# The shift and scale columns of the first norm, summed on TensorE in four column groups of the array

## The chip, the core and the metric

The kernel runs on one of the eight cores of a Trainium2 chip. A core has TensorE (matrix products, PE in the profile; its weight loads are PEld), VectorE (DVE), ScalarE (ACT), GpSimd (POOL) and SyncE (SP, which here only issues transfers), on-chip memory of 128 partitions (SBUF), a memory of eight banks per partition into which TensorE writes its products (PSUM), and 16 DMA engines that bring data from the chip's main memory. The metric is the device time of one execution in microseconds (us); less is better.

## The reference

A trunk of two residual layers over 256 tokens of 2048 features, in float32. The first layer mixes with a gated MLP over chunks of tokens beside a convolution, the second with attention; each then has an MLP of 8192 hidden channels. Every norm is modulated by a conditioning vector c:

```python
c_act = jax.nn.silu(c)
for l in range(DEPTH):
    mod = c_act @ ada_w[l] + ada_b[l]          # [2048] @ [2048, 12288]
    shift1, scale1, gate1, shift2, scale2, gate2 = jnp.split(mod, 6, axis=-1)
    h = _modulate(_rms(x, norm1_g[l]), shift1, scale1)   # rms * (1 + scale) + shift
    mix = _even_mixer(h, ...) if l % 2 == 0 else _mla_mixer(h, ...)
    x = x + gate1 * mix
    h = _modulate(_rms(x, norm2_g[l]), shift2, scale2)
    x = x + gate2 * (square(relu(h @ mlp_w1[l])) @ mlp_w2[l])
```

Each of the six vectors of a layer is a product of one row with 2048 x 2048 of ada_w, 16 MiB of weights that are used once. This document is about shift1 and scale1 of the first layer: nothing of the first mixer's projection can start without them.

## The kernel before

**Weights.** `wraw` (lines 111 to 122) loads a tile of 512 rows by 512 columns, 1 MiB, as four blocks of 128 rows on the 128 partitions, on SyncE's queue. Tiles for conditioning lie in the pool `raw` (four buffers), tiles that are multiplied as whole float32 (`gemm32`, lines 147 to 156) in `wh` (three buffers).

**Conditioning.** `ada_quarters` (lines 246 to 276) makes two columns side by side, shift (j0) and scale (j0 + 1), 512 features at a time: a quarter is eight steps, each with one tile. A step has four product-sums on VectorE, one for each block of 128 rows (lines 267 and 269): the accumulator `accq` [128, 512] gets the block times the 128 values of c that belong to it, one to a partition. After four tiles of a column `ada_finish_col` (lines 216 to 223) has to sum `accq` over the partitions: TensorE transposes its four blocks of 128 columns into PSUM (`transpose4`, lines 102 to 108), VectorE reduces them along the free axis (line 221) and adds the bias (line 223). The result is feature-major: 128 features on the partitions, four columns for a quarter.

**The first stage** (`even`, lines 474 to 505). Four steps are issued, then x is loaded and its squares summed by ScalarE (`setup_x`, lines 897 to 905), two more steps, then `setup_vectors` (lines 907 to 918), which transposes small vectors (biases, norm gains) that ScalarE's queue has loaded as rows (`vr`, lines 877 to 893). `tc.issue_after(self.last)` queues instructions of the block behind the named one where they run on its engine. When a quarter of the columns is there, `norm_start`'s generator gives, for both halves of the tokens, the normed x transposed (line 355) with the shift and gain columns, and ScalarE writes the modulated, transposed features (line 500). Then three tiles of the projection are multiplied (lines 503 to 505): 24 float32 products a quarter, 128 x 128 by 128 x 512. In the profile their outputs are called mm and pa.

**Order.** A framework orders the instructions of each engine by the program and by its own estimate of readiness, and sets all waits. While `gemm32` asks for a weight tile, `side_work` (lines 135 to 145) takes steps off the conditioning queue, here 8/3 to a tile; so a quarter's three weight tiles are followed by two, three and three steps for the next quarter, ahead of the tile's products in the program. `ada_until` takes as many as are still wanting.

PSUM has four buffers for products (`mm`), two for transposes and small things (`tr`) and two more (`ms`).

After this stage come the rest of the projection (`gemm32` too), with the gate of the first mixer and the next shift and scale computed beside it, and then the rest of the trunk.

Of the kernel before, what the change touches and what calls it, by code (L numbers as in the profile page):

```python
# [9 lines left out]
F32 = mybir.dt.float32  # L10
# [3 lines left out]
ALU = mybir.AluOpType  # L14
AX = mybir.AxisListType

P = 128
D = 2048
T = 256
NH = T // P  # L20
KB = D // P
# [21 lines left out]
class Trunk:  # L43
    def __init__(self, ctx, tc, t):
# [17 lines left out]
        self.first = 0  # tiles still to be split by GpSimd  # L62
# [5 lines left out]
    def rsqrt(self, out, v):  # L68
        """out = v ** -0.5 for v > 0: a first guess from the bits, a third-order step, a Newton step."""
# [14 lines left out]
        # out <- 8/3 of its third-order step, then Newton with the 8/3 taken out again  # L84
# [7 lines left out]
    def split(self, src, hi, lo, engine=None):  # L92
        """src = hi + lo, both with the 12 significant bits that one pass of the array takes."""
        self.nc.scalar.copy(hi, src)  # L94
        (engine or self.nc.vector).tensor_tensor(lo, src, hi.bitcast(F32), op=ALU.subtract)  # L95
# [6 lines left out]
    def transpose4(self, srcs):  # L102
        """Up to four [128, n] blocks -> one PSUM bank, transposed side by side."""
        ps = self.tr.tile([P, 512], F32, tag="tr", name="trp")
        for i, s in enumerate(srcs):
            w = s.shape[-1]
            self.nc.tensor.transpose(ps[:w, i * P : i * P + s.shape[0]], s, self.ident[: s.shape[0], : s.shape[0]])  # L107
        return ps

# [14 lines left out]
    def wtile(self, w, k0, nk, n0, nw):  # L124
# [3 lines left out]
        # VectorE is busy with the norm when a phase's first tiles come: GpSimd splits those  # L128
# [6 lines left out]
    def side_work(self, size=1.0):  # L135
        """Work that is spread beside the weight tiles: conditioning and the convolution."""
# [10 lines left out]
    def gemm32(self, ps, x, w, g, n0):  # L147
        """ps += x[:, 512 features of group g] @ w[those, n0:n0+512], whole float32 passes."""
# [12 lines left out]
    def gemm(self, x, xk0, w, k0, nkb, n0, nw, skew=False):  # L161
        """[256, nw] = x[:, K] @ w[K, n0:n0+nw], as two PSUM tiles of 128 tokens; with skew the
        first half of the tokens is complete well before the second."""
# [25 lines left out]
    def gemm_quarter(self, units, x, q, paired):  # L189
        """512 features of x into each of units = (psum, w, n0, nw); with paired, the first half of  # L190
        the tokens of two units goes before their second half."""
# [23 lines left out]
    # mod = silu(c) @ ada_w + ada_b, one 1 MiB piece of ada_w to a step  # L215
    def ada_finish_col(self, out, layer, j, q, acc):
        """Feature-major column sums of acc [128, 512], plus the bias."""
# [7 lines left out]
    def ada_col(self, layer, j):  # L225
        """self.mod[layer, j] = [128, 16], feature-major."""
# [19 lines left out]
    def ada_quarters(self, layer, j0, side=None, aided=0):  # L246
        """Columns j0 and j0 + 1 side by side, complete for 512 features after every eight steps.
        The first aided quarters go by ScalarE and GpSimd, with room for products in side."""
# [28 lines left out]

    def ada_row(self, layer, j, side=None):
        """self.mod[layer, j] = [128, 2048], the same in every partition. With side = [128, 4096],
        the products go to ScalarE and the sums to GpSimd."""  # L280
# [37 lines left out]
    def at_end(self, last):  # L318
        """Before the last product of a stage: no more work beside it."""
        self.hold = last  # L320
        return last

    def ada_more(self, rate, *lists):
        """Steps to be worked off beside the coming weight tiles, rate steps to a tile."""
        for l in lists:
            self.ada_queue.extend((rate, step) for step in l)
# [24 lines left out]
    def norm_t(self, h, q, r):  # L351
        """Four blocks of (x * r).T in PSUM."""
# [4 lines left out]
    def norm_start(self, layer, which):  # L357
        """A function that gives 512 features' (shift, gain) columns: modulate(rms(x) * g) = x * rstd * gain + shift."""
# [14 lines left out]
    def norm_quarter(self, quarter, q, pair):  # L373
        """512 features of h.T, as (hi, lo)."""
# [10 lines left out]
    def norm_mod(self, layer, which):  # L385
        """h.T (hi, lo) of modulate(rms(x) * g, shift, scale)."""
# [6 lines left out]
    def gated(self, src, gate, h, c):  # L393
        """x[:, chunk] += gate * src, for one half"""
# [6 lines left out]
    def residual(self, ps, gate, c, last, part=None):  # L401
        """x[:, chunk] += gate * (ps + part)"""
# [16 lines left out]
    def mlp(self, layer, last):  # L419
# [8 lines left out]
        # the first three chunks take the features as the modulation completes them  # L428
# [9 lines left out]
        # sums over the blocks of hidden channels  # L438
# [35 lines left out]
    def even(self, layer):  # L474
# [5 lines left out]
        self.ada_more(8 / 3, self.ada_quarters(layer, 0))  # L480
        self.ada_steps(X_AT)
        self.setup_x()
        self.ada_steps(V_AT - X_AT)
        with self.tc.issue_after(self.last):
            self.setup_vectors()
# [3 lines left out]
        # mixer B  # L489
# [34 lines left out]
        def glu(j, pa, pg):  # L524
# [8 lines left out]
            def tap(b, k):  # L533
                # read from PSUM, which leaves GpSimd its port to SBUF
# [9 lines left out]
            # two sums side by side, so that no tap waits on the one before  # L544
# [11 lines left out]
        # mixer A  # L556
# [46 lines left out]
        def layer_norm():  # L603
            """LayerNorm over channels (the partition axis), swish."""
# [24 lines left out]
        # mixer A's rows of the first three chunks, then mixer B's  # L629
# [18 lines left out]
    def rms_columns(self, srcs):  # L648
        """1 / rms along the free axis of each of some [128, n], as the columns of one tile."""
# [18 lines left out]
    def low_rank(self, src, r, gcol, pair, k0, h):  # L668
        """One half's [128, 512], scaled by its rms r and by g, transposed and split."""
# [11 lines left out]
    def rope(self, out, src, tab, n):  # L681
        """Rotary pairs of [128, n, 64]; tab = [128, 128]: (C1 | C2), (-S2 | S1)."""
# [8 lines left out]
    def odd(self, layer):  # L691
# [12 lines left out]
        # columns 512:1088 = c_kv and the rotary key, as pieces of 320 and 256 columns  # L704
# [21 lines left out]
        # two heads at a time: keys, values and queries, then scores, then the output, a step apart  # L726
# [10 lines left out]
        def squares(c, s, src):  # L737
            """Sums of squares of [P, half, head, n], as row s of three."""
# [20 lines left out]
        def normalized(c):  # L759
# [8 lines left out]
            # rotary pairs of both halves  # L768
# [16 lines left out]
        def scores(c):  # L785
# [3 lines left out]
            for i in range(2):  # L789
                rows = slice(i * ROPE, (i + 1) * ROPE)  # L790
                sc = self.ms.tile([P, 512], F32, tag="ms", name="sc")
                # query block 1 sees 256 keys, query block 0 the first 128
# [18 lines left out]
        def weights_t(ss):  # L811
            out = []
            for s in ss:
                # transposed: keys 0..127 for query blocks 0 and 1, keys 128..255 for block 1
# [45 lines left out]
    def setup(self):  # L860
# [9 lines left out]
        nc.vector.tensor_copy(self.cT, ps[:, :KB])  # L870
        one = self.tmp.tile([P, P], F32, tag="t512", name="one")
# [4 lines left out]
        # 128-long rows that become per-partition columns  # L876
# [43 lines left out]
    def setup_even(self):  # L920
        nc, t, c = self.nc, self.t, self.const
        # conv taps: rows (tap, block) -> columns
# [12 lines left out]
        # spatial weights, lower triangle, transposed  # L935
# [10 lines left out]
    def setup_odd(self, room):  # L946
        """Mask and rotary tables, with room [128, 768] for the raw ones."""
        nc, t = self.nc, self.t
        # causal mask: query block 1 on 256 keys, then query block 0 on 128
# [9 lines left out]
        # rotary tables of both halves with the head gains  # L959
# [39 lines left out]
def rope_table():  # L999
    """cos | sin of the rotary angles, [256, 64]: by shape alone."""  # L1000
# [23 lines left out]
```

## Time and profile before

| what | value |
|---|---|
| device time, median of three runs | 2189.13 us |
| lowest and highest | 2187.72, 2189.61 us |
| span of the profiled execution | 2185.9 us |
| TensorE busy (products), share | 2090.9 us, 96% |
| VectorE busy, share | 1564.9 us, 72% |
| ScalarE busy, share | 932.3 us, 43% |
| GpSimd busy, share | 146.7 us, 7% |
| data moved | 567.70 MB, mean 260 GB/s |

The profiled execution's own device time is not listed apart from its span. The span runs from the first instruction to the last; the median of the runs is 3.2 us above it, launch and end included.

How to read the rows. A row of the timeline gives start, length in us, engine, line, operation, output<-inputs, how many instructions are merged in it, and in brackets the idle time before it and what ended that. SPq and ACTq are the queues that issue transfers. A row of the groups gives line, engine, operation, names, shapes and count, then busy time, the mean of one in ns, and the idle time just before with what ended it. `PE` records of products overlap: a record ends later than the next one starts, so a rate is read from starts. Some of the first page's rows, in 40 equal slices of 54.6 us, show the first stage in the first two or three digits:

```profile
PE   2889999899999999999998999989999999999999
DVE  6849999888777878787767878766656545554555
DMA  9999968899898899989755646647778556556653
GB/s 350 384 346 330 332 242 295 275 317 339 315 337 315 329 326 319 339 304 334 270 174 174 211 158 214 229 154 250 256 271 264 178 192 189 189 192 192 189 191 122
```

### The profile page before, as it was taken

How to read it: one execution, taken by the hardware profiler on the slowest of the kernel's cores; microseconds unless marked ns; L12 is line 12 of the kernel's file. 1: busy time of each engine (PE TensorE's matmuls, PEld its weight loads, DVE VectorE, ACT ScalarE, POOL GpSimd, SP SyncE). 2: the span in 40 equal slices, each digit the busy share in tenths (PEclk: the TensorE clock that was granted, in tenths of full speed). 3: DMA queues.
4: the chain of work that ended last, by engine and by line, in shares of the span. 5: the costliest groups of instructions: out<-in, count | busy, mean ns of one | idle time of the engine just before them, and what ended most of it. 6: DMA issues, size and time to landing. Idle time of an engine off the chain costs nothing.

```text
span 2185.9 us, 23655 instructions
## 1 busy us (share of the span) xinstructions
PE 2090.9 (96%) x9138; PEld 1635.7 (75%) x9138; DVE 1564.9 (72%) x1763; ACT 932.3 (43%) x1184; POOL 146.7 (7%) x95
## 2 busy tenths in 40 slices
PE   2889999899999999999998999989999999999999
PEld 1444458678888888888888787868888888888887
DVE  6849999888777878787767878766656545554555
ACT  2135435444444334333436776444434433433432
POOL 0038710000000000000001000010000000000000
PEclk9999999899999999999999999989999999999999
DMA  9999968899898899989755646647778556556653
GB/s 350 384 346 330 332 242 295 275 317 339 315 337 315 329 326 319 339 304 334 270 174 174 211 158 214 229 154 250 256 271 264 178 192 189 189 192 192 189 191 122
DMA packets 238620, 567.70 MB, mean 260 GB/s; under 512 B 9150, under 2 KB 17784, under 8 KB 221864
## 3 DMA queue, kind: packets, MB, share of 16 engines
q1 hardware_dynamic: 236288, 562.60, 74.3%
q10 hardware_dynamic: 1564, 2.28, 0.3%
q8 instruction: 72, 1.18, 0.2%
q0 software_dynamic: 656, 1.31, 0.2%
q14 instruction: 40, 0.33, 0.0%
HBM read 564.06 MB, written 2.10 MB: 259 GB/s over the span
## 4 chain that ended last, share of the span: by engine, by line
PE 85%; DVE 9%; DMA 5%; ACT 1%; issue 1%; SPq 0%; ACTq 0%; DVEq 0%
PE mm L183 23%; PE mm L184 23%; PE mm L185 23%; PE mm L153 4%; DMA raw<-in_ada_w 4%; PE trp L107 3%; DVE accq L269 2%; DVE cvsq L542 1%; DVE wl L95 1%; PE mm L210 1%; PE mm L211 1%; PE mm L212 1%; PE sc L797 1%; PE sc L796 1%; DMA raw<-in_mlp_w 1%
## 5 line engine op out<-in xcount | busy, mean ns | idle before, releaser
L95 DVE TENSOR_TENSOR wl<-raw,wh 128x2048 fp32r<-128x2048 f32 (+2 forms) x312 | 704.7, 2259 | 424.0 <-PE mm L184 317.9
L94 ACT CAST wh<-raw 128x2048 fp32r<-128x2048 f32 (+3 forms) x316 | 596.6, 1888 | 774.1 <-PE mm L185 515.2
L183 PE MATMUL mm<-wh,f_h 128*128 128x512 f32 x1024 | 399.6, 390 | 0.0
L185 PE MATMUL mm<-wh,f_l 128*128 128x512 f32 x1024 | 399.3, 390 | 0.0
L184 PE MATMUL mm<-wl,f_h 128*128 128x512 f32 x1024 | 398.7, 389 | 0.0
L185 PE MATMUL mm<-wh,h_l 128*128 128x512 f32 (+2 forms) x928 | 358.2, 386 | 0.0
L183 PE MATMUL mm<-wh,h_h 128*128 128x512 f32 (+2 forms) x928 | 358.2, 386 | 0.0
L184 PE MATMUL mm<-wl,h_h 128*128 128x512 f32 (+2 forms) x928 | 357.0, 385 | 0.6 <-DVE wl L95 0.6
L185 PEld LDWEIGHTS mm<-wh,f_l 128*128 128x128 f32 x1024 | 192.2, 188 | 39.8
L184 PEld LDWEIGHTS mm<-wl,f_h 128*128 128x128 f32 x1024 | 192.3, 188 | 39.6
L183 PEld LDWEIGHTS mm<-wh,f_h 128*128 128x128 f32 x1024 | 192.3, 188 | 39.2
L184 PEld LDWEIGHTS mm<-wl,h_h 128*128 128x128 f32 x928 | 175.0, 189 | 34.0 <-DVE wl L95 1.1
L185 PEld LDWEIGHTS mm<-wh,h_l 128*128 128x128 f32 x928 | 174.9, 188 | 33.4
L183 PEld LDWEIGHTS mm<-wh,h_h 128*128 128x128 f32 x928 | 175.0, 189 | 32.7
L153 PE MATMUL mm<-raw,x 128*128 128x512 f32 x448 | 195.7, 596 | 1.0 <-ACT x L500 0.6
L269 DVE SCALAR_TENSOR_TENSOR accq<-raw,cT,accq 128x512 f32<-128x512 f32 x210 | 153.7, 749 | 16.6 <-DMA raw<-in_ada_w 13.3
L153 PEld LDWEIGHTS mm<-raw,x 128*128 128x128 f32 x448 | 84.6, 191 | 104.6 <-issue 98.5
L237 DVE SCALAR_TENSOR_TENSOR acc<-raw,cT,acc 128x2048 f32<-128x2048 f32 x60 | 140.8, 2346 | 9.7 <-DMA raw<-in_ada_w 9.7
L297 DVE SCALAR_TENSOR_TENSOR acc<-raw,cT,acc 128x2048 f32<-128x2048 f32 x48 | 112.7, 2347 | 4.4 <-DMA raw<-in_ada_w 4.4
L542 DVE SCALAR_TENSOR_TENSOR cvsq<-yp,convw,cvsq 128x256 f32<-128x256 f32 x240 | 96.0, 476 | 0.0
L303 POOL TENSOR_TENSOR side<-side 128x1024 f32<-128x1024 f32 x32 | 74.8, 2361 | 19.3 <-ACT side L302 19.3
L452 ACT ACTIVATE relu<-mm 128x512 f32<-128x512 f32 x60 | 35.8, 599 | 87.7 <-PE mm L185 81.5
(270 smaller groups left out, 2246.9 us busy)
## 6 DMA issues: line engine op xcount, KB each, us to landing
raw<-in_mlp_w SPq DMA_DIRECT2D x256, 1024.0 KB, 5.6
raw<-in_ada_w SPq DMA_DIRECT2D x192, 1024.0 KB, 5.4
raw<-in_ab_w_in SPq DMA_DIRECT2D x32, 1024.0 KB, 9.7
raw<-in_ab_w_out SPq DMA_DIRECT2D x16, 1024.0 KB, 8.3
raw<-in_mla_w_out SPq DMA_DIRECT2D x16, 1024.0 KB, 4.9
raw<-in_mla_w_ukv SPq DMA_DIRECT2D x8, 1024.0 KB
raw<-in_mla_w_uq SPq DMA_DIRECT2D x8, 768.0 KB, 4.8
raw<-in_mla_w_in SPq DMA_DIRECT2D x4, 1024.0 KB, 7.2
```

The source lines that it names most:

```text
L94: self.nc.scalar.copy(hi, src)
L95: (engine or self.nc.vector).tensor_tensor(lo, src, hi.bitcast(F32), op=ALU.subtract)
L107: self.nc.tensor.transpose(ps[:w, i * P : i * P + s.shape[0]], s, self.ident[: s.shape[0], : s.shape[0]])
L153: self.nc.tensor.matmul(ps[h], x[:, 4 * g + k, h * P : (h + 1) * P], raw[:, k, :], start=g + k == 0, stop=4 * g + k == KB - 1,)
L183: nc.tensor.matmul(o, a, hi[:, i, :nw], start=first, stop=False)
L184: nc.tensor.matmul(o, a, lo[:, i, :nw], start=False, stop=False)
L185: nc.tensor.matmul(o, b, hi[:, i, :nw], start=False, stop=last)
L237: nc.vector.scalar_tensor_tensor(acc, raw, self.cT[:, kb : kb + 1], acc, op0=ALU.mult, op1=ALU.add)
L269: self.last = nc.vector.scalar_tensor_tensor(acc, raw[:, k, :], c, acc, op0=ALU.mult, op1=ALU.add).ins
L297: nc.vector.scalar_tensor_tensor(acc, raw, c, acc, op0=ALU.mult, op1=ALU.add)
L303: nc.gpsimd.tensor_tensor(acc[:, sl], acc[:, sl], prod, op=ALU.add)
L542: nc.vector.scalar_tensor_tensor(o, y, wk, o, op0=ALU.mult, op1=ALU.add)
```

## The change

The new `ada_quarters_pe` takes the place of `ada_quarters` for the first layer's first two columns; other uses of `ada_quarters` stay. In a step TensorE multiplies each of the four blocks of 128 rows with its 128 values of c, repeated into 32 columns, and writes to 32 partitions of one PSUM bank: block k of every tile goes to partitions 32k to 32k + 31. The four tiles of a column accumulate there. Then ScalarE copies the bank to SBUF, TensorE multiplies each block of 128 columns with a vector `sel` that is one on partitions 0, 32, 64 and 96 (this adds the four groups and turns the features onto the partitions), and VectorE adds the bias. The steps of a column now follow each other (`q, i, g` in place of `q, g, i`). `setup_vectors` is called first, since the bias add needs it, and `issue_after` names ScalarE's copy. `sel` is a sum over the identity's columns 0, 32, 64 and 96.

```diff
+    def ada_quarters_pe(self, layer, j0):
+        nc = self.nc
+        box = {}
+
+        def step(q, i, g):
+            if (q, i, g) == (0, 0, 0):
+                for j in (j0, j0 + 1):
+                    self.mod[layer, j] = self.const.tile([P, KB], F32, tag=f"mod{layer}{j}", name=f"mod{layer}{j}")
+            if g == 0:
+                box["acc"] = self.tr.tile([P, 512], F32, tag="tr", name="adap")
+            acc = box["acc"]
+            raw = self.wraw(self.t["ada_w"][layer], 4 * g, 4, (j0 + i) * D + q * 512, 512)
+            for k in range(4):
+                rows = slice(32 * k, 32 * k + 32)
+                nc.tensor.matmul(acc[rows], self.cT[:, 4 * g + k : 4 * g + k + 1].broadcast_to([P, 32]), raw[:, k, :], start=g == 0, stop=g == 3)
+            if g == 3:
+                rows = self.tmp.tile([P, 512], F32, tag="t512", name="adar")
+                self.last = nc.scalar.copy(rows, acc).ins
+                ps = self.tr.tile([P, 512], F32, tag="tr", name="adac")
+                for k in range(4):
+                    nc.tensor.matmul(ps[:, k : k + 1], rows[:, k * P : (k + 1) * P], self.sel, start=True, stop=True)
+                b0 = layer * 96 + (j0 + i) * KB + 4 * q
+                nc.vector.tensor_tensor(
+                    self.mod[layer, j0 + i][:, 4 * q : 4 * q + 4], ps[:, :4], self.ada_b[:, b0 : b0 + 4], op=ALU.add
+                )
+                if i == 1:
+                    self.quarters[layer, j0] = q + 1
+
+        self.quarters[layer, j0] = 0
+        return [lambda q=q, g=g, i=i: step(q, i, g) for q in range(4) for i in range(2) for g in range(4)]
...
     def even(self, layer):
...
-        self.ada_more(8 / 3, self.ada_quarters(layer, 0))
+        self.setup_vectors()
+        self.ada_more(8 / 3, self.ada_quarters_pe(layer, 0))
         self.ada_steps(X_AT)
         self.setup_x()
-        self.ada_steps(V_AT - X_AT)
-        with self.tc.issue_after(self.last):
-            self.setup_vectors()
         self.ada_until(lambda: self.quarters[layer, 0] > 0)
...
     def setup(self):
...
         nc.vector.tensor_copy(self.cT, ps[:, :KB])
+        self.sel = c.tile([P, 1], F32, name="sel")
+        nc.vector.tensor_reduce(self.sel, self.ident.rearrange("p (a b) -> p a b", b=32)[:, :, 0], axis=AX.X, op=ALU.add)
```

## The prediction

> **What bounds the kernel now.** I read the page first, then the busy windows of its first 170 us, then TensorE's timeline there, because the change touches nothing later.
>
> ```profile
> span 2185.9 us, 23655 instructions
> PE 85%; DVE 9%; DMA 5%; ACT 1%; issue 1%; SPq 0%; ACTq 0%; DVEq 0%
> raw<-in_ada_w SPq DMA_DIRECT2D x192, 1024.0 KB, 5.4
> ...
> 50.00:60.00 10.00, 10.00 (x25) 4.40 (x24) 9.68 (x15) 0.00 (x0) 0.00 (x0) 1.00 1.05 387
> 60.00:70.00 10.00, 7.01 (x20) 3.13 (x18) 9.43 (x15) 0.00 (x0) 0.00 (x0) 1.00 1.05 387
> 80.00:90.00 10.00, 7.16 (x17) 2.85 (x15) 8.01 (x11) 0.00 (x0) 0.00 (x0) 1.00 1.05 387
> 110.00:120.00 10.00, 7.02 (x16) 2.84 (x16) 7.50 (x11) 0.00 (x0) 0.00 (x0) 1.00 1.05 387
> 130.00:140.00 10.00, 9.29 (x30) 4.76 (x31) 1.03 (x4) 3.11 (x9) 1.55 (x2) 1.00 0.93 330
> ```
>
> The chain that ended last is 85% TensorE; over the whole span this is a TensorE kernel. In a window row stand the stretch and its length, then the busy time of PE, PEld, DVE, ACT and POOL, PE's granted clock, the DMA share and GB/s. In the four rows up to 120 us the DMA engines are full at 387 GB/s, VectorE is busy for 75 to 97% and TensorE has idle time. One tile of 1024 KB takes 1.049 MB / 387 GB/s = 2.71 us. A quarter of the features needs eight tiles of ada_w and three of ab_w_in: 11 x 2.71 = 29.8 us.
>
> ```profile
> 45.24 14.46 PE L153 MATMUL mm<-raw,x 128*128 128x512 f32 x32
> ...
> 72.75 14.41 PE L153 MATMUL mm<-raw,x 128*128 128x512 f32 x32
> 90.57 6.25 PE L153 MATMUL pa<-raw,x 128*128 128x512 f32 x10 [3.41 <-DMA raw<-in_ab_w_in]
> ...
> 102.32 7.13 PE L153 MATMUL mm<-raw,x 128*128 128x512 f32 x16 [0.29 <-ACT x L500]
> ...
> 120.72 6.26 PE L153 MATMUL pa<-raw,x 128*128 128x512 f32 x10 [3.71 <-DMA raw<-in_ab_w_in]
> 126.82 0.60 PE L107 MATMUL trp<-ident,accq 128*128 128x128 f32 x4
> 127.25 2.74 PE L153 MATMUL pa<-raw,x 128*128 128x512 f32 x6
> ...
> 132.45 14.00 PE L153 MATMUL mm<-raw,x 128*128 128x512 f32 x32 [0.29 <-ACT x L500]
> 146.29 7.03 PE L153 MATMUL pa<-raw,x 128*128 128x512 f32 x16
> 153.25 0.33 PE L107 MATMUL trp<-ident,cwr 62*128 62x62 f32 x2
> ```
>
> The four quarters start their products at 45.24, 72.75, 102.32 and 132.45: the last two periods are 29.6 and 30.1 us, the DMA's 29.8. TensorE waits 3.4 and 3.7 us for weights in the two middle ones. So in this stage the transfers set the pace, VectorE comes next, and TensorE has slack. From 132.45 on it has none:
>
> ```profile
> 190.00:210.00 20.00, 20.00 (x48) 8.85 (x47) 19.92 (x52) 10.96 (x13) 18.49 (x10) 1.00 0.90 328
> ```
>
> Whatever moves the end of the fourth quarter's products (now 153.25) moves the rest of the kernel with it, since TensorE is then full, and VectorE's convolution starts from these products too.
>
> **The change part by part.** *Removed from VectorE:* 128 product-sums, and eight reductions of transposed sums.
>
> ```profile
> L269 DVE SCALAR_TENSOR_TENSOR accq<-raw,cT,accq 128x512 f32<-128x512 f32 x120 | 88.2, 750 | 16.0 <-DMA raw<-in_ada_w 13.3
> L153 PE MATMUL mm<-raw,x 128*128 128x512 f32 x448 | 195.7, 596 | 1.0 <-ACT x L500 0.6 <-DMA raw<-in_ab_w_in 0.4
> L153 PE MATMUL pa<-raw,x 128*128 128x512 f32 x64 | 32.0, 654 | 7.1 <-DMA raw<-in_ab_w_in 7.1
> 51.39 0.19 PEld L153 LDWEIGHTS mm<-raw,x 128*128 128x128 f32 x1 [0.24 <-issue]
> 51.82 0.19 PEld L153 LDWEIGHTS mm<-raw,x 128*128 128x128 f32 x1 [0.24 <-issue]
> ```
>
> That is 88 us of VectorE for 120 of them, all beside transfers. Its worth is the delay between the last tile's landing and the first product, counted below; the 30 us period itself does not shrink.
>
> *Added to TensorE.* Line 153 calls 32 tiles x 8 = 256 float32 products, and has 448 + 64 = 512 records: a product is two passes, each with its own weight load, started 0.43 us apart (51.39, 51.82). A quarter's 24 products are 48 passes and take 153.25 - 132.45 = 20.8 us. The new sum has 4 products of the same 512 columns in a step, 32 a quarter: 64 passes. Only 32 columns of the array are used by each, but a pass streams the same 512 columns of data. No row of before has two passes side by side, so the price has two ends:
> - all one after another, as the passes of line 153: 64 x 0.43 = 27.5 us a quarter;
> - all four column groups at once: 16 x 0.43 = 6.9 us.
>
> I take a value between. The two passes of one product fall on the same columns and must follow each other; the queue holds both passes of the first group, then both of the second. If a pass cannot start before the one ahead of it in the queue (no row here shows one overtaking), the second group's first pass runs beside the first group's second, and so on: two passes at a time, 32 x 0.43 = 13.8 us. A run of steps also has an unpaired pass at its end; at 8/3 steps to a weight tile there are three runs a quarter: 1.3 us.
>
> The Trainium skill, "TensorE: Matmul & The Clock Gate", Part 3, says that matmuls in different column groups overlap, with starts about 4 ns apart, that three groups gave 2.38 times, and that matmuls start and end strictly in program order. By its span formula alone a step would cost little more than its two passes, the first rival below with its 2187 to 2191 us; by its order rule, with the two passes that line 153 shows, it is the pairing and 2216 us. No row of before shows either. "TensorEngine Tiling (Array Packing)", Tiling Modes, speaks against the change: a change of the tiling mode drains TensorE, and here there would be six changes a quarter. The trace of before has no such change to time; if each cost the 0.16 us by which a record of line 153 (596 ns) outlasts its 0.43, three quarters would be 2.9 us longer, 2219 us.
>
> *The new finish* of a column: ScalarE's copy out of PSUM, four products with one column, a bias add.
>
> ```profile
> L520 ACT COPY a<-mm 128x512 f32<-128x512 f32 x2 | 1.1, 588 | 0.1
> 39.19 0.16 DVE L223 TENSOR_TENSOR mod<-mod,ada_b 128x4 f32<-128x4 f32 x1
> 42.34 0.16 DVE L367 SCALAR_TENSOR_TENSOR A<-mod,vecs 128x4 f32<-128x4 f32 x1
> 44.63 0.81 ACT L500 ACTIVATE x<-trp,mod,A 128x128 f32<-128x128 f32 x2 [17.83 <-PE trp L107]
> ```
>
> The four products are eight passes, each with a full 128-column weight load as a transpose has it; four transposes pass in 127.25 - 126.82 = 0.43 us, so 0.107 us a pass, 0.86 us a column, 1.7 us a quarter. They replace eight transposes (0.86 us). The eight transposes of x stay: 0.86 us. The added wait is TensorE's for the copy: 0.59 us and two handovers, twice a quarter. Behind it in TensorE's queue stand the next steps and products of weight tiles, which VectorE and ScalarE wait for. Nothing prices it exactly: between nothing, where products of a weight tile are placed in it, and 2 us a quarter. I take 1.2 us, for this and for idle time where the array's shape changes. The two PSUM buffers that sums, finish and transposes now share lie in the same 0 to 2 us.
>
> *The start.* What decides it is when the eighth tile lands.
>
> ```profile
> 6.73 0.48 DVE L267 TENSOR_SCALAR accq<-raw,cT 128x512 f32<-128x512 f32 x1 [1.63 <-DMA raw<-in_ada_w]
> 11.33 0.49 DVE L267 TENSOR_SCALAR accq<-raw,cT 128x512 f32<-128x512 f32 x1 [3.32 <-DMA raw<-in_ada_w]
> 13.83 9.56 SPq L118 DMA_DIRECT2D raw<-in_ada_w  x4
> 39.31 0.75 DVE L269 SCALAR_TENSOR_TENSOR accq<-raw,cT,accq 128x512 f32<-128x512 f32 x1
> ...
> 10.00:12.00 2.00, 0.00 (x0) 0.01 (x1) 0.67 (x2) 0.30 (x1) 0.00 (x0) 1.00 0.19 69
> 12.00:14.00 2.00, 0.73 (x3) 0.45 (x3) 2.00 (x4) 0.00 (x0) 0.00 (x0) 1.00 0.73 201
> 14.00:16.00 2.00, 0.00 (x0) 0.00 (x0) 0.46 (x1) 0.00 (x0) 0.00 (x0) 1.00 1.05 400
> 12.02 0.73 PE L107 MATMUL trp<-ident,vr 106*128 106x106 f32 x3 [7.13 <-DMA vr<-in_mla_kv_norm_g]
> SPq L118 <- DMA raw<-in_ada_w: 9.1, 1, 9.1
> ```
>
> SyncE waits 9.1 us for a landing, and there is a hole in the transfers up to about 13.8 us. Two tiles of ada_w have landed by then (VectorE opens their sums at 6.73 and 11.33). I see nothing that would fill the hole, so six tiles and the two of x follow: 13.8 + 8 x 2.71 = 35.5 us. Before, VectorE was still summing at 39.3 and the first product started at 45.24. After: 35.5 + the last step's rest 0.9 + copy 0.6 + finish 1.1 + bias add and gain 0.3 + activation 0.5 + about 1.4 of handovers = 40.3 us. The row statistics are ready by then, since VectorE is idle. So 4.9 us are won here.
>
> *Moved:* setup_vectors goes ahead of the sums: three transposes, two copies, one small product, no DMA. On TensorE's queue the sums now stand behind the transposes, which wait for vr until 12.02; the first tile lands near 6.7, so the first step starts near 12.8. Its buffer comes free at 13.7 to 16.2, against SyncE's 13.83 for the fifth tile's issue; the tiles of x, which need no such buffer, lie between and keep the queue filled. I cost it at nothing; without that cover it would be up to 2.4 us. The column selector's reduction is some 0.2 us on an idle VectorE: nothing.
>
> *Sum.* A quarter on TensorE: 20.8 + 13.8 + 1.3 + 1.7 + 0.9 + 1.2 = 39.7 us, more than the DMA's 29.8: TensorE becomes the bound of the stage. End of the fourth quarter: 40.3 + 3 x 39.7 + 20.8 = 180.2, against 153.25: 26.9 us later. The span becomes 2212.8; the median of 2189.13 is 3.2 above the span, and I keep that: **2216 us**. With 0 to 2 us for waits and 0 to 0.1 us of extra per pair, this case is 2209 to 2229.
>
> **The rivals.**
> *All four groups at once (it does not get slower).* For it: the four groups share neither columns nor output partitions. Against it: each has two passes, and the second group's come behind both of the first's. The quarter is 20.8 + 6.9 + 1.7 + 0.9 + 1.2 = 31.5, or 30.3 without waits; with the first product at 39.5 the end is 151.2 to 154.8, 2187 to 2191 us: the start's gain is paid back, nothing is left. It decides from a step of about 0.9 us. It cannot do much better, since 29.8 is the DMA's floor: 39.5 + 89.4 + 20.8 = 149.7, 2185.6.
> *The groups don't run at once (the change doesn't do what it says).* For it: every row of before has one pass after another. Then a step is 3.43 us, more than the DMA's 2.71; the eighth tile's step ends at 40.9, the first product starts at 45.5, a quarter is 20.8 + 27.5 + 1.7 + 0.9 + 1.2 = 52.1, the end 45.5 + 156.3 + 20.8 = 222.6: 2258 us, up to 2266 with waits.
>
> **How the numbers follow.** Two at a time 0.55, one at a time 0.26, all at once 0.13, 0.06 for other orders of work that I have not seen (halved between the signs). The range 2197 to 2266 leaves out four at once and little else. Two executions differ by up to 2 us and 0.2% is 4.4 us, about what a measurement of this kernel can tell from no change: four at once falls mostly within it (0.10), with a little beyond. So slower 0.83, same 0.11, faster 0.06.
>
> **What would show it.** TensorE's busy time in 50 to 130 us full and its waits for ab_w_in gone; the DMA share below 1.05; steps 1.7 us apart where they run together (0.9 or 3.4 for the rivals); first product near 40 us; quarters 39.7 apart; the transposes of cwr near 180. I am wrong if the passes are issued in another order than product by product, if the granted clock falls, or if the later stages absorb the delay.

## The result, and the profile after

The changed kernel takes 2204.9 us (median of four runs, 2202.44 to 2205.48) where the kernel before takes 2189.37 beside it (2187.72 to 2189.76): ratio 1.007, 95% interval 1.0057 to 1.0084, so 15 us or 0.7% slower. The profiled execution has a span of 2203.8 us, 17.9 above the profile of before. From the page, the rows that answer to those of before:

```profile
span 2203.8 us, 24110 instructions
PE 2130.5 (97%) x9426; PEld 1641.0 (74%) x9426; DVE 1470.7 (67%) x1628; ACT 936.0 (42%) x1192; POOL 146.4 (7%) x95
PE 85%; DVE 6%; DMA 6%; ACT 1%; POOL 1%; issue 1%; SPq 0%; ACTq 0%; DVEq 0%; POOLq 0%
```

VectorE lost 94 us of work (1564.9 to 1470.7) and TensorE gained 40 (2090.9 to 2130.5). The chain is TensorE's in both. The busy windows of the first stage say what that exchange did there:

```profile
30.00:40.00 10.00, 7.68 (x36) 2.91 (x29) 0.33 (x2) 0.58 (x1) 0.00 (x0) 0.50 1.05 387
40.00:50.00 10.00, 10.00 (x32) 4.08 (x34) 0.00 (x0) 2.90 (x8) 0.00 (x0) 0.82 1.05 386
80.00:90.00 10.00, 10.00 (x40) 3.10 (x32) 0.00 (x0) 0.00 (x0) 0.00 (x0) 1.00 0.89 295
110.00:120.00 10.00, 10.00 (x40) 3.07 (x39) 0.00 (x0) 1.56 (x5) 0.97 (x2) 1.00 0.87 294
130.00:140.00 10.00, 10.00 (x41) 3.23 (x40) 0.00 (x0) 0.46 (x1) 0.00 (x0) 1.00 0.52 189
```

From 40 us on TensorE is busy all the time but for one wait of 0.76 us, and from 80 us on the DMA engines are no longer full: 295, 294 and 189 GB/s in rows that had 387, 387 and 330. VectorE has next to nothing to do in that time. The bound has moved from the transfers to TensorE. TensorE's timeline gives the size of it (adap are the new sums, adac the small products of their finish):

```profile
34.79 1.94 PE L294 MATMUL adap<-raw,cT 128*32 128x512 f32 x8 [0.79 <-DMA raw<-in_ada_w]
...
40.96 4.94 PE L153 MATMUL mm<-raw,x 128*128 128x512 f32 x8
45.83 1.06 PE L294 MATMUL adap<-raw,cT 128*32 128x512 f32 x8
...
76.05 3.70 PE L153 MATMUL mm<-raw,x 128*128 128x512 f32 x8
...
109.18 3.70 PE L153 MATMUL mm<-raw,x 128*128 128x512 f32 x8
112.81 1.06 PE L294 MATMUL adap<-raw,cT 128*32 128x512 f32 x8
113.80 1.98 PE L153 MATMUL mm<-raw,x 128*128 128x512 f32 x4
...
140.31 0.95 PE L300 MATMUL adac<-sel,adar 128*128 128x1 f32 x8
141.12 1.07 PE L107 MATMUL trp<-ident,xn 128*128 128x128 f32 x8
142.31 14.00 PE L153 MATMUL mm<-raw,x 128*128 128x512 f32 x32
...
163.11 0.33 PE L107 MATMUL trp<-ident,cwr 62*128 62x62 f32 x2
```

The quarters start at 40.96, 76.05, 109.18 and 142.31: the first product comes 4.3 us earlier than before (45.24), the periods are 35.1, 33.1 and 33.1 us instead of 27.5, 29.6 and 30.1, and the fourth quarter's products end at 163.11 instead of 153.25. So 9.9 of the 15 us arise in the stage that was changed, and some 5 behind it. The experiments go after both. The "some 5" goes by the medians; in the two profiles, one execution each, it is 8 us.

One step, all eight passes of four products, is 0.99 us from start to start (112.81 to 113.80). How they lie shows in narrow windows on the tile adap, where the first count is of PE records alive in the stretch and the second of weight loads:

```profile
45.80:45.90 0.10, 0.07 (x4) 0.08 (x8) 0.00 (x0) 1.00 1.09 410
45.90:46.00 0.10, 0.10 (x4) 0.08 (x8) 0.00 (x0) 1.00 1.06 389
46.20:46.30 0.10, 0.10 (x8) 0.00 (x0) 0.00 (x0) 1.00 1.01 369
```

Four passes start in the first stretch, and all eight weight loads begin there. Four more passes start between 46.20 and 46.30, when the modelled ends of the first four (some 0.6 us after their starts) are not reached. The single records start at 45.825, 45.832, 45.838 and 45.845, then at 46.277, 46.284, 46.292 and 46.298. All four column groups run at once, 7 ns apart, and a step is two such rounds. (The records don't name their group; that the four are of four groups follows from one_group below, where passes of one group never overlap.) That is the rival to which the prediction gave 0.13.

### The profile page after: what moved, and what is told of

Read it like the earlier page. It is cut to its first block, busy times and chain, and to the rows that moved or that the text cites. A ratio compares the mean times of both kernels' runs of the same rounds, so it can differ in the third digit from the quotient of the medians.

```text
span 2203.8 us, 24110 instructions
## 1 busy us (share of the span) xinstructions
PE 2130.5 (97%) x9426; PEld 1641.0 (74%) x9426; DVE 1470.7 (67%) x1628; ACT 936.0 (42%) x1192; POOL 146.4 (7%) x95
## 4 chain that ended last, share of the span: by engine, by line
PE 85%; DVE 6%; DMA 6%; ACT 1%; POOL 1%; issue 1%; SPq 0%; ACTq 0%; DVEq 0%; POOLq 0%
PE mm L183 22%; PE mm L184 22%; PE mm L185 22%; PE mm L153 6%; DMA raw<-in_ada_w 4%; PE trp L107 3%; DMA raw<-in_mlp_w 2%; DVE wl L95 1%; PE adap L294 1%; PE mm L210 1%; PE mm L211 1%; PE pa L153 1%; PE mm L212 1%; DVE cvsq L573 1%; PE sc L828 1%; DVE accq L269 1%
## 5 line engine op out<-in xcount | busy, mean ns | idle before, releaser
L184 PEld LDWEIGHTS mm<-wl,f_h 128*128 128x128 f32 x1024 | 192.2, 188 | 39.8
L185 PEld LDWEIGHTS mm<-wh,f_l 128*128 128x128 f32 x1024 | 192.2, 188 | 39.8
L237 DVE SCALAR_TENSOR_TENSOR acc<-raw,cT,acc 128x2048 f32<-128x2048 f32 x60 | 140.9, 2349 | 40.6 <-DMA raw<-in_ada_w 40.4
```

Of the source, the lines that this page charges most:

```text
L184: nc.tensor.matmul(o, a, lo[:, i, :nw], start=False, stop=False)
L185: nc.tensor.matmul(o, b, hi[:, i, :nw], start=False, stop=last)
L237: nc.vector.scalar_tensor_tensor(acc, raw, self.cT[:, kb : kb + 1], acc, op0=ALU.mult, op1=ALU.add)
```

## Experiments

Times of before were measured beside each kernel's, on the same chip. "Stage end" is the start of the first transpose of cwr, 153.25 us in before.

**How many passes run at once.** Four kernels change which columns of the array the sums use; the copy, the finish and the flags that open and close a sum are fitted to that (not shown).

```diff
# one_group: all four blocks of rows into one group
-                rows = slice(32 * k, 32 * k + 32)
+                rows = slice(0, 32)
# full_array: one product of 128 columns for each block
-                nc.tensor.matmul(acc[rows], self.cT[...].broadcast_to([P, 32]), raw[:, k, :], ...)
+                nc.tensor.matmul(acc, self.cT[...].broadcast_to([P, P]), raw[:, k, :], ...)
# two_alternate: groups 0, 1, 0, 1
+                rows = slice(32 * (k % 2), 32 * (k % 2) + 32)
# two_blocked: groups 0, 0, 1, 1
+                rows = slice(32 * (k // 2), 32 * (k // 2) + 32)
```

> All four blocks of a step go to the same 32 columns of the array, one after another into 32 partitions, and the copy and the finish take only these 32 partitions. If what makes a step 0.99 us is that four different column groups work at once, a step has eight passes of 0.43 us in a row, about 3.55 us; the stage's quarter grows from 33.1 by 8 x 2.5 to about 53 us, the first product comes near 45 us, the fourth quarter's products end near 225 us, and the time is about 2266 us. Rival: a product with 32 columns is cheaper by itself, whatever group it goes to; then a step stays near 1.0 us and the time near 2205 us.

> c is repeated into all 128 columns, so that a step is four ordinary products over the whole array, accumulated in the same 128 partitions, and the finish picks partition 0. A step is eight passes of 0.43 us, 3.43 us. If the 0.3 us that each visit costs beyond its passes comes from the change between the column groups and the whole array, it vanishes here: a quarter of about 50 us and about 2258 us, some 7 us less than with all blocks in one group. If it comes from breaking up the run of the projection's products, it stays: about 2266 us as with one group.

> Blocks 0, 1, 2, 3 go to column groups 0, 1, 0, 1; the copy and the finish take 64 partitions. Both theories of the order give four slots of 0.43 us, a step of about 1.85 us with the change of shape: a quarter of about 40 us, and about 2227 us.

> Blocks 0, 1, 2, 3 go to column groups 0, 0, 1, 1. If TensorE starts a pass as soon as its column group is free, past a waiting pass of another group, this costs the same as 0, 1, 0, 1: a step of about 1.85 us and 2227 us. If passes start in the order of the queue, only the last of group 0 has the first of group 1 beside it: six or seven slots, a step of 2.7 to 3.1 us, a quarter of 47 to 50 us and 2248 to 2256 us. The rival to both, that the second pass of a product follows its first directly and holds up all that stand behind, gives seven slots here and would have given five slots, 2.1 us, for the changed kernel's own step, which took 0.99.

| kernel | time, us (one execution each; before 2184.7) | first product | quarters, us | stage end |
|---|---|---|---|---|
| one_group | 2261.4 | 47.74 | 53.6, 52.7, 56.3 | 233.97 |
| full_array | 2260.6 | 47.25 | 52.2, 51.3, 55.7 | 229.87 |
| two_alternate | 2224.5 | 39.60 | 41.1, 40.3, 40.2 | 181.97 |
| two_blocked | 2223.5 | 39.99 | 41.1, 40.4, 40.2 | 182.53 |

In one group nothing overlaps, so the rival, that a product with 32 columns is cheaper by itself, is out. The timeline of one_group has two steps (16 passes) between products:

```profile
49.65 7.05 PE L294 MATMUL adap<-raw,cT 128*32 128x512 f32 x16
56.63 5.42 PE L153 MATMUL mm<-raw,x 128*128 128x512 f32 x12
```

That is 6.98 us or 0.44 a pass. The timeline of two_blocked has one step where one_group's has two:

```profile
39.99 3.70 PE L153 MATMUL mm<-raw,x 128*128 128x512 f32 x8
43.62 1.92 PE L294 MATMUL adap<-raw,cT 128*32 128x512 f32 x8
45.47 1.13 PE L153 MATMUL mm<-raw,x 128*128 128x512 f32 x2
46.52 1.92 PE L294 MATMUL adap<-raw,cT 128*32 128x512 f32 x8
```

43.62 to 45.47 is 1.85 us; two_alternate has 1.84 (43.24 to 45.08). So the time goes by the number of groups, about 3.5, 1.85 and 0.99 us a step with one, two and four. It does not go by the order in which the kernel lists the products. In two_blocked both products of the first group stand ahead of the second group's, and yet the narrow windows on adap show the groups side by side from the first pass:

```profile
46.50:46.60 0.10, 0.08 (x2) 0.08 (x4) 0.00 (x0) 1.00 1.14 430
46.90:47.00 0.10, 0.10 (x4) 0.02 (x2) 0.00 (x0) 1.00 0.93 348
```

Two passes start in the first stretch; the second holds them and the next two. The records start at 46.523 and 46.536, then 46.976 and 46.989; since passes of one group don't overlap, each pair has one of either group. The prediction's reason for pairing had two parts: that the queue holds the passes product by product, and that none starts before the one ahead of it. They can't both be true. Which one fails, whether the build or the array's queue puts the passes side by side, the runs don't tell.

full_array against one_group prices the change of the array's shape. Both sum one product after another, but the sums of full_array have the 128 columns of the products around them. Its quarters are 1.4, 1.4 and 0.7 us shorter by the rows, for 13 visits to the sums in three quarters: 0.27 us a visit. Ahead of the last quarter full_array also waits longer for ScalarE, 4.19 us against 3.73; without that it is 0.31. The times, one execution each, differ by 0.8 us where some 7 had been expected, so this price rests on the timelines. The rows of after say the same: the step from 112.81 to 113.80 has 0.13 us over its two rounds of 0.43, and the eight passes from 109.18 to 112.81 have 0.19 over theirs: 0.32 us a visit, both sides counted. What TensorE does in that time the rows don't show.

**Fewer visits.** Two steps at a time, in pairs, halve the visits.

```diff
+            box[g % 2] = raw
+            if g % 2 == 0:
+                return
+            for g2 in (g, g - 1):
             for k in range(4):
...
```

> The changed kernel, but the products of two steps are issued together (the later step's first, since its tile lands last), so that TensorE goes to the column groups four times a quarter and not eight. If a visit costs 0.3 us beyond its passes, 12 visits less after the first product save 3.6 us: a quarter of about 31.9 us and 2201 us. If the visits cost nothing by themselves and the quarter's 33.1 us have another cause, the time stays at 2205 us; if holding two tiles longer starves the transfers, it rises.

pairs: 2199.9 us (before 2187.56), ratio 1.0056, 1.0043 to 1.0068. Its timeline:

```profile
111.89 1.92 PE L298 MATMUL adap<-raw,cT 128*32 128x512 f32 x16
113.75 4.56 PE L153 MATMUL mm<-raw,x 128*128 128x512 f32 x10
...
133.53 1.92 PE L298 MATMUL adap<-raw,cT 128*32 128x512 f32 x16
136.22 1.05 PE L304 MATMUL adac<-sel,adar 128*128 128x1 f32 x8 [0.76 <-ACT adar L301]
...
138.31 14.00 PE L153 MATMUL mm<-raw,x 128*128 128x512 f32 x32
159.11 0.33 PE L107 MATMUL trp<-ident,cwr 62*128 62x62 f32 x2
```

16 passes take 1.86 us where two visits of eight took 1.98, and the stage ends 4 us earlier than in after. That is the time that was expected, but not by the way that was expected: 2.9 of the 4 us come from the first product (39.67) and the first quarter (33.5 us where after has 35.1); the other two quarters are 32.6 us where 31.9 was forecast. In the third, the products and sums of the four visits saved take 1.4 us less by the rows, 0.36 a visit, and most of it goes back to a wait: no product is left to lie behind the last step, so TensorE stands still for ScalarE's copy (0.76 us, above). TensorE is still the bound, so it stays slower than before.

**The start alone, and the sums by halves.** moved_only is the kernel before with `setup_vectors` ahead of the sums. half gives the first quarter and all of scale to TensorE, and leaves shift's other quarters on VectorE.

```diff
# moved_only
+        self.setup_vectors()
         self.ada_more(8 / 3, self.ada_quarters(layer, 0))
...
# half, in the step
+            if i == 0 and q > 0:
+                # four product-sums into box["sum"] on VectorE
...
+                return
```

> The kernel before, with nothing changed but that the small vectors are set up first. I costed the move at nothing: 2189 us, within 2 us. If it delays VectorE's first sums, which start at 6.7 us, until the vectors' transposes at 12 us, the time is up to 5 us longer.

> The first quarter as in the changed kernel; in the other three the shift column is summed by VectorE as before and the scale column, which comes second, by TensorE. TensorE's quarter is 33.1 less four visits of 1.3 us and less half of a finish: about 28 us, under the 29.8 of the transfers. If the changed kernel loses because TensorE became the bound of the stage, this one is bound by transfers again, with a first product at 41 us and a shorter way from the last tile to the products: the fourth quarter's products end at 150 to 153 us and the time is 2185 to 2189 us, the time of before or a little less. If the loss comes from something else in the change (the moved vectors, the copy and finish, PSUM), about half of it remains: 2195 to 2200 us.

> The changed kernel once more, for a second profile and more times. The stage's end should be at 163 us again and the median at 2205 us. If the further 8 us that its first profile shows after that stage belong to the change, the second profile shows the same waits in the same places; if they are the transfers' luck in one execution, they move or shrink, and the median lies below the first profile's 2205.5 us.

moved_only: 2188.24, ratio 1.0 (0.9992 to 1.0009), stage end 153.25. The move costs nothing, as predicted. half: 2192.62, ratio 1.0019 (1.0011 to 1.0028), between the two times that were expected. after_again, the changed kernel once more on that chip: 2202.74, ratio 1.0069 (1.0057 to 1.0081). Its profile has the stage's end at 164.09 and a span of 2201.5: behind the stage it loses 4.8 us against before's profile, not 8, so some of the 8 belonged to one execution. The timeline of half, and a row of its windows:

```profile
41.14 15.37 PE L153 MATMUL mm<-raw,x 128*128 128x512 f32 x32
...
132.61 14.00 PE L153 MATMUL mm<-raw,x 128*128 128x512 f32 x32
153.41 0.33 PE L107 MATMUL trp<-ident,cwr 62*128 62x62 f32 x2
```

```profile
110.00:120.00 10.00, 8.63 (x34) 3.21 (x34) 5.18 (x9) 0.00 (x0) 0.00 (x0) 1.00 1.05 387
```

With the first product 4.1 us earlier than before and 30.1 to 30.9 us a quarter, half ends the stage where before ends it. The transfers set that pace (387 GB/s, as in before): the fourth quarter's weights come when they come. What made after's stage longer, then, is that TensorE became its bound, and the early start is worth nothing even where TensorE has slack. But half is about 4 us slower though its stage is not longer. Something behind the stage costs as well.

**The order of the next stage's transfers.** Beside the next weight tiles (W) run steps for the gate's row, one tile each (r), and other columns (a). The planner spreads them by its count of steps and its estimates, and the new steps shift that. The issues on SyncE's queue, from the last weight tiles of the stage on:

```
before, moved_only  WrrWaWrWraWrrWaWrWraWrWrWaWr...
after, half         WrWraWrWraWrWrWaWrrWaWrWrWar...
before_late         WrWraWrWraWrWrWaWrrWaWrWraWr...
pairs               WrrWaWrWraWrWrWarWrWaWrWraWr...
half_early2         WrrWarWrWaWrWrWarWrWaWrWrWar...
after_order, half_order  WrrWaWrWraWrWrWaWrrWaWrWrWar...
```

before_late is the kernel before with one thing changed: the second r may be issued only behind the next W. The rest of the order follows by the planner's own rules.

```diff
         def step(kb):
-            raw = self.wraw(self.t["ada_w"][layer], kb, 1, j * D, D)
+            if side is not None and kb in (1,):
+                with self.tc.issue_after(self.wdma):
+                    raw = self.wraw(self.t["ada_w"][layer], kb, 1, j * D, D)
+            else:
+                raw = self.wraw(self.t["ada_w"][layer], kb, 1, j * D, D)
```

half_early2 is half with two steps taken ahead (`self.ada_steps(2)` after the gate row is queued).

> The kernel before with one edge added on SyncE's queue: the second tile of the gate's row (kb = 1) is issued behind the first weight tile of the stage after the first, and no longer ahead of it. The order of that stage's transfers is then nearly that of the changed kernel, whose planner put the tile there too; all else is the kernel before. If this order is what costs the changed kernel some 5 us after the first stage, this kernel has 2191 to 2193 us with the first stage's end still at 153.3. If the 5 us have another cause, it stays at 2187.6, the median that 23 runs of before had last.

> The kernel with half of the sums on TensorE, and two steps of the gate's row taken in the program ahead of the second stage, so that the second tile of the row is issued ahead of the next weight tile, as in the kernel before. If that order is what the half kernel loses after its first stage (which ends where that of before ends), its time falls from 2192.6 to about 2188 us. If not, it stays at 2192 to 2193 us.

before_late: 2193.07 (before 2186.78), ratio 1.0027, 1.0018 to 1.0036: 6 us slower with the stage ending at 153.37. half_early2: 2201.9, ratio 1.0068 (1.0054 to 1.0083), a miss: it moved the third, fourth and seventh r one place ahead too, and later steps with them, and lost 15 us with the stage's end at 153.25. So what happens behind the stage can cost as much as the change does, with nothing lost in the stage itself. Where the loss of before_late first shows is the gate, which needs the whole row. SyncE's issues, VectorE's first gated tile and the mixer's first product in the timelines of before:

```profile
164.50 0.37 SPq L118 DMA_DIRECT2D raw<-in_ab_w_in  x1
164.96 0.93 SPq L116 DMA_DIRECT2D raw<-in_ada_w  x2
171.37 0.38 SPq L118 DMA_DIRECT2D raw<-in_ab_w_in  x1
...
273.83 1.48 DVE L95 TENSOR_TENSOR gl<-side,gh 128x512 fp32r<-128x512 f32 x1
...
304.51 2.08 PE L593 MATMUL pm<-vu,wsT 128*128 128x128 f32 x8
```

and of before_late:

```profile
164.35 0.37 SPq L118 DMA_DIRECT2D raw<-in_ab_w_in  x1
164.81 0.46 SPq L116 DMA_DIRECT2D raw<-in_ada_w  x1
171.22 0.37 SPq L118 DMA_DIRECT2D raw<-in_ab_w_in  x1
171.68 0.46 SPq L116 DMA_DIRECT2D raw<-in_ada_w  x1
...
277.21 0.68 DVE L95 TENSOR_TENSOR gl<-side,gh 128x512 fp32r<-128x512 f32 x1
...
307.53 1.23 PE L598 MATMUL pm<-vu,wsT 128*128 128x128 f32 x4
```

An r (line 116) that stood with its neighbour at 164.96 is issued at 171.68, the first gated tile comes 3.4 us later, and pm 3.0. In the changed kernel the same rows are:

```profile
287.12 2.19 DVE L95 TENSOR_TENSOR gl<-side,gh 128x512 fp32r<-128x512 f32 x1 [2.48 <-ACT gh L94]
...
317.40 0.79 PE L624 MATMUL pm<-vu,wsT 128*128 128x128 f32 x2
```

Counted from the stage's end that is 124.0 and 154.3 us, against 120.6 and 151.3 in before and 123.8 and 154.2 in before_late. A second execution of the same kernel, after_again, has 122.9 and 153.2, so about 1 us of this is no difference of kernels.

The last two kernels put the second r back where before has it, without touching the rate of the later steps:

```diff
         self.ada_more(R0, mixed)
+        self.ada_steps(2)
+        self.ada_credit += -2.0
```

> The changed kernel with one difference: the second tile of the gate row is asked for ahead of the second weight tile of the next stage, as in the kernel before, and the rate of the later steps is unchanged, so that the end of the first stage stays at 163 us. If the place of that tile costs what it cost in the kernel before (6.3 us there), the loss of 15 us falls to 9 or 11: 2197 to 2200 us with the kernel before at 2187 to 2189. If the place of that tile is a small part of it, and the later steps of the row or the delay itself are what costs, it stays at 2203 to 2205.

> The kernel with half of the sums on each engine, whose first stage ends as early as before (153.4 us) and which lost 4 us, with the same one difference in the order. If the order of the next stage's transfers is all that it lost, it comes to the time of the kernel before: 2186 to 2189 us, ratio 0.999 to 1.001. If something else of the split costs, it stays at 2191 to 2193.

after_order: 2201.6 (before 2187.81), ratio 1.0062, 1.0049 to 1.0074. half_order: 2191.83, ratio 1.0021, 1.0012 to 1.0031. Neither bears out the order theory in this form: half_order stays within the rival's 2191 to 2193, and after_order lies between the two ranges, its interval overlapping that of after_again. The gate of half_order does come earlier, by its timeline

```profile
276.35 2.18 DVE L95 TENSOR_TENSOR gl<-side,gh 128x512 fp32r<-128x512 f32 x1 [2.49 <-ACT gh L94]
...
306.41 0.80 PE L638 MATMUL pm<-vu,wsT 128*128 128x128 f32 x2
```

122.7 and 152.8 us after its stage's end (153.63) where half has 124.5 and 154.5, but the time doesn't follow. All runs together, with the loss taken from the ratio, or, where there is one execution, from the difference to before:

| kernel | stage end against before | loss by the ratio | rest |
|---|---|---|---|
| moved_only (order of before) | 0.0 | 0.0 | 0.0 |
| before_late | +0.1 | 5.9 | 5.8 |
| half | +0.2 | 4.2 | 4.0 |
| half_order | +0.4 | 4.6 | 4.2 |
| pairs | +5.9 | 12.3 | 6.4 |
| after | +9.9 | 15.3 | 5.4 |
| after_again | +10.8 | 15.1 | 4.3 |
| after_order | +10.8 | 13.6 | 2.8 |
| half_early2 | 0.0 | 14.9 | 14.9 |
| two_alternate (one execution) | +28.7 | 39.8 | 11.1 |
| two_blocked (one execution) | +29.3 | 38.8 | 9.5 |
| full_array (one execution) | +76.6 | 75.9 | -0.7 |
| one_group (one execution) | +80.7 | 76.7 | -4.1 |

The intervals of the ratio are 2 us to either side or more, and the stage's end differs by 1 us between two executions of after, so the rests of 3 to 6 us can't be told from one another. The single executions are rougher still: before alone ranges over 7 us (2183.89 to 2191.11 in 23 executions). Even so the rest is no fixed price: it goes from about -4 us, where the stage is 81 us longer, to 15. What is shown: before_late loses some 6 us by order alone, and the one kernel with the order of before, moved_only, loses nothing. What is not shown: that the rest of after is all order. Its second r alone is not the cause; after_order and half_order still differ from before from the fifth weight tile on, and no kernel here has the new sums with the whole order of before. No version tried beats the kernel before.

## Why the prediction came out as it did

The forecast, 2216 us with slower at 0.83, had the sign and, within its range, the time. The mechanism that it held likeliest was not the one that ran, so that the time came out near is in part luck: two errors lay on opposite sides.

**Two passes at a time: wrong, and this is the step that failed.** The prediction priced a step at 1.72 us (32 x 0.43 for eight steps, and 1.3 us a quarter for unpaired ends) and said that only one group's pass could run beside the other's because the queue holds them product by product. Four run at once: 0.99 us. two_alternate and two_blocked show the stage that the forecast described, but only because they have two groups: their third quarter is 40.2 us where 39.7 was forecast, and their stage ends at 182.0 and 182.5 where 180.2 was. Their time is not the forecast's even so: 39 us above their own before, where 26.9 was forecast. The Trainium skill, "TensorE: Matmul & The Clock Gate", Part 3, has starts about 4 ns apart in different column groups; here they are 7 ns apart. It also says that packed products start strictly in program order; the starts of two_blocked are not in the order in which the kernel lists the products, and the order that the build made of them is not in the trace.

**The terms of a quarter**, third quarter of after, from start to start of the timeline's rows:

| term | forecast | four at once | measured |
|---|---|---|---|
| 48 passes of weight tiles | 20.8 | 20.8 | 22.4 |
| sums | 13.8 + 1.3 | 6.9 | 8.0 |
| finish | 1.7 | 1.7 | 1.6 |
| transposes of x, with the wait for their activation | 0.9 | 0.9 | 1.2 |
| waits for the copy | 1.2 | 0 to 1.2 | 0 |
| sum | 39.7 | 30.3 to 31.5 | 33.1 |

The rival's quarter was 1.6 to 2.8 us short, and nearly all of it lies at the changes of shape: 1.6 us in the passes of the weight tiles and 1.1 in the sums. The forecast assumed three visits to the sums a quarter, from 8/3 steps to a tile; the planner spread the eight steps to eight visits, each with about 0.3 us at its edges. The price that it tried on one row (0.16 us a change, two to a visit: 0.32 us) is the one measured, but that is chance: the row was the length of a product's record, whose end is modelled, and no change of shape. The count was wrong, 16 changes a quarter and not six. The Trainium skill, "TensorEngine Tiling (Array Packing)", Tiling Modes, says that a change of the mode drains TensorE; the trace agrees that it costs something, and 0.3 us a visit is the price here.

**TensorE becomes the bound: right.** 33.1 us a quarter against the transfers' 29.8, full busy windows, a DMA share of 0.87 to 0.89. The rival of four at once expected a tie, with the start's gain paying for the difference; with 33.1, and a first product at 40.96 where that rival had 39.5, it is a loss of 9.9 us.

**The start: near in size, worth nothing by itself.** First product 40.96, forecast 40.3, with errors that cancel. The eighth step starts at 34.79 by the timeline, against 35.5 for the eighth tile's landing. What was not counted is the clock: the row 30:40 has it at 0.50, and the step at 34.79 takes twice its time (1.94 us); the first eight passes of products take 4.94 instead of 3.70. The prediction had named a falling clock as a sign that it was wrong. two_alternate, whose steps are longer (granted clock 0.89 in that row), has its first product at 39.60, ahead of the changed kernel. The Trainium skill, "TensorE: Matmul & The Clock Gate", Part 1, lets the clock fall to half after an idle stretch; the trace agrees, with a wait of 4.97 us for a tile ahead of the step at 26.75 and a granted clock of 0.66 from 20 to 30 us. half shows that the 4 us bought nothing: the transfers run at 387 GB/s from before the first product on, in before as in half, and the last tiles land no earlier. So the floor of 149.7 us that the prediction reckoned from an earlier first product is not reached.

**The move of the vectors: right**, nothing (moved_only, 0.9992 to 1.0009).

**The delay passes to the end undiminished: wrong by some 5 us.** The forecast added the 26.9 us of the stage to the time and nothing else. Here 9.9 became 15. The prediction said that the change touches nothing later; it touches the planner, and the next stage's transfers came in another order. before_late shows that such an order can cost this much; that it is what cost it here stays open. Too long a step and a cost that was not seen fell on opposite sides, and so the number was only 11 us off.

**Smaller slips.** Of the four window rows up to 120 us one, 50 to 60 us, has TensorE full. No waits at all would make the forecast 2212, not the 2209 at the low end of its span. And two executions of before differ by up to 7 us, not 2.

## What to carry to other kernels

Float32 products of 32 columns in four column groups cost about as much as two passes of one product (0.99 us against 0.86), and with two groups the order in which they are listed made no difference; but count the visits, since every visit among full products costs about 0.3 us. Keep them together, but leave a product to lie behind the last one, or TensorE waits for the copy. An engine that has slack of a few us a period is a poor place for 10 us of work a period: compare its new sum with the period before moving anything to it. And where a planner spreads work, compare the issue orders of both kernels far behind the change before believing that the rest only shifts.

## What the runs showed of the hardware

- Four column groups: passes 7 ns apart, rounds 0.45 and then 0.54 us long (45.825 to 46.277 to the next full product at 46.82); all eight weight loads of a step begin within its first 0.1 us.
- Two groups give 1.85 us a step in either listing of the products, one group 3.5 us; a pass of 32 columns takes the 0.43 us of a pass of 128.
- A visit to the column groups among full products costs 0.3 us beyond its passes (0.31 from full_array and one_group, 0.32 from the rows of after).
- A step of narrow passes that comes every 2.7 us, with waits of 0.7 to 0.8 us between, leaves the granted clock at 0.50 (30 to 40 us), and the first products behind it pay 1.2 us.
